# gMLP: u by seven block products a chunk pair, spatial mixing as fp32 products, modulation steps in two out-projections

## The chip, the cores and the metric

One core of one Trainium2 chip runs the whole program. The time is device microseconds of one execution; the kernel before has a median of 2796.57 us over three runs (2794.27 to 2799.32). TensorE (PE) multiplies, VectorE (DVE) and ScalarE (ACT) work elementwise, GpSimd (POOL) and SyncE (SP) issue DMAs, POOL also reduces over partitions.

## The reference, cut to what matters

Two layers over 512 latent and 256 context tokens (768 rows of width 1024, all fp32). Each layer is FFN, token mixer, FFN; every sub-layer is modulated by shift, scale and gate that come from a conditioning vector. The mixer of layer 0 is the one that changes:

```python
def gmlp_mix(h, w_in, sgu_g, sgu_b, w_s, b_s, w_out):      # h: (1, T, 1024)
    u, v = jnp.split(jax.nn.gelu(h @ w_in, approximate=False), 2, axis=-1)   # 3072 each
    v = layer_norm(v, sgu_g, sgu_b)
    v = v.reshape(b_, t_ // 128, 128, 8, 384)
    v = jnp.einsum('gpq,bnqgc->bnpgc', w_s, v) + b_s.T[None, None, :, :, None]
    return (u * v.reshape(b_, t_, 3072)) @ w_out
m = jax.nn.silu(cond) @ w_mod + b_mod                       # modulation, nine vectors a layer
```

The spatial product mixes the 128 tokens of a chunk of tokens with one 128x128 matrix w_s for each of eight groups of 384 channels.

## The kernel before, in words

**Precision.** Matrix products run on fp32r data. Each fp32 operand is split into a high part (an ACT cast) and a low part (a DVE subtraction), and each product is made of three: high x high, high x low, low x high (`split`, `split_later`, `product`). So every weight tile costs a cast of 128x512 on ACT and a subtraction of 128x512 on DVE. Where text says "the low part of a weight", this subtraction is meant.

**Sub-layers.** In order: FFN 0, gMLP, FFN, FFN, attention, FFN. An FFN and gMLP's v use a seven-product scheme (Strassen and Winograd's) over blocks of h: features in two halves, tokens in two halves of 384. Its operands made from h are called B11, T1, T2, B21, T3, B22, T4 (`combine`) and its weight sums come from four raw tiles g1, u1, u2, g2 (job kind "s" in `units`, lines 327 to 359: four DVE operations on the raw tiles, L334, L337, L345, L353, and seven splits). One tile makes 7 x 12 = 84 matmuls of 128x384.

**gMLP.** First the v stage: v for all tokens, written to DRAM (`v_spill`), with statistics for its norm. Then the u stage, a loop over 24 chunks j of 128 channels. A chunk (a) makes u by eight plain block products a token half (`project`, 96 matmuls of 128x384 for two chunks, weight jobs "u": two raw tiles a chunk, no sums); (b) fetches v's chunk from DRAM on SP's queue, scales it by the norm on ACT (`normed`, six operations of 128x128) and splits it (ACT 128x768, DVE 128x768); (c) mixes it (`spatial`): w_s, transposed and split, is a moving operand of 256 columns, v's high and low parts are the weights, 12 matmuls; (d) adds the two halves with gain and bias on DVE (six operations of 128x256), applies gelu to u on ACT and multiplies; (e) does one or two modulation steps. The results of the last KEPT = 4 chunks are split and stay on chip, those of the others go to DRAM by POOL's queue.

**Out-projections.** `out_proj` runs over the rows of the weights f (24 in gMLP, 22 in an FFN), once for each half of 512 output columns. A row is 6 token blocks x 3 = 18 matmuls of 128x512. Rows in DRAM are read back by POOL's queue (`feed`), split three rows ahead (`prepare`, AHEAD = 3), and weights are made up to eight tiles ahead (W_BUFS). The second half keeps READ_BACK = 10 rows from the first. DVE also does the residual (z by ln_g and ln_b) there.

**Modulation.** w_mod is not multiplied on TensorE: a modulation step (`mod_unit`, called by `fill`) loads 256 KB of w_mod on SP's queue and adds it, times one element of the conditioning vector, into an accumulator on DVE, once for each of two vectors. A unit (layer, index) has 16 steps; after eight, POOL reduces the accumulator over partitions. MOD_PLAN says which units belong to which sub-layer; what is left of them at the sub-layer's end is done there at once. Steps are placed by calls of `fill` in the loops.

**What sets the order.** From `pin(True)` on, every engine runs its instructions in the order in which the program writes them. `slot` sets it after each block product: low parts of weights waiting, an early copy, up to two new weight tiles, then the step's own work.

## Time and profile before

| | us |
|---|---|
| median of three runs | 2796.57 |
| the profiled execution | 2794.23 |
| its span on the chip | 2790.9 |
| TensorE busy | 2746.1 (98%) |
| DVE busy | 2078.2 (74%) |
| ACT busy | 1294.0 (46%) |
| u stage, first product to the out-projection's first | 732.78 to 970.40 |

Times in the views count from the span's start. L89 is the line of a helper that pins operations, so nearly every row has it; rows are told apart by the names out<-in: `ps<-comb,w` are block products on h, `ps<-w_sT,vn` spatial products, `ps<-w,acts` out-projections, `acc<-mraw` modulation steps. PE is TensorE's matmul, PEld its weight load, which overlaps. A matmul's own time contains its latency; what one costs in a row of many is the distance from start to start.

### The profile page before, as it was taken

To read this page: it belongs to the slowest core of one execution; us is meant where nothing else is said; L and a number is where in the kernel's file an instruction comes from. 1 tells how busy PE (TensorE), PEld (TensorE's weight loads), DVE (VectorE), ACT (ScalarE), POOL (GpSimd) and SP (SyncE) were. 2 spreads that over 40 slices of the span, in tenths; PEclk is the share of its full clock that TensorE was granted. 3 is DMA by queue.
4 is the path that set the end of the run, shared out by engine and by line. 5 is a ranking of instruction groups with operands and counts; after the bars stand their busy time and mean duration, and the time that the engine had idled before them with its cause. 6 is when DMAs were issued, how large, how long until landed. Compare 5 with 4: busy or idle time off the path is not lost.

```text
span 2790.9 us, 41006 instructions
## 1 busy us (share of the span) xinstructions
PE 2746.1 (98%) x14370; PEld 2481.2 (89%) x14370; DVE 2078.2 (74%) x3601; ACT 1294.0 (46%) x2559; POOL 548.6 (20%) x620
## 2 busy tenths in 40 slices
PE   7999999999999999999999999999999999999998
PEld 5999988888899988899998889999988888888887
DVE  6879989587798876587898659789896698733445
ACT  6544442475655432564444246444432666623321
POOL 1002144212111241100314120013242121000001
PEclk9999999999999999999999999999999999999999
DMA  7444466377766483344456534454594424354352
GB/s 234 142 138 143 138 235 207 111 223 231 220 191 178 131 291 108 119 148 148 137 146 218 174 105 144 144 147 141 170 313 148 148 72 91 130 151 130 112 170 87
DMA packets 408133, 447.31 MB, mean 160 GB/s; under 512 B 29560, under 2 KB 289080, under 8 KB 407928
## 3 DMA queue, kind: packets, MB, share of 16 engines
q1 hardware_dynamic: 371848, 332.77, 38.3%
q0 software_dynamic: 36080, 111.93, 13.2%
q8 instruction: 112, 1.84, 0.3%
q14 instruction: 93, 0.76, 0.1%
HBM read 382.62 MB, written 64.19 MB: 160 GB/s over the span
## 4 chain that ended last, share of the span: by engine, by line
PE 65%; DVE 3%; ACT 2%; issue 2%; POOL 1%; DMA 0%; SPq 0%; DVEq 0%; POOLq 0%; ACTq 0%
PE ps L89 64%; PE pp L89 1%; ACT h L692 0%; POOL rs L203 0%; ACT z L2228 0%; ACT p L1743 0%; DVE nm L1735 0%; DVE z L89 0%; DVE q L1640 0%; DMA mraw<-in_w_mod_dram 0%; POOL acc L474 0%; DVE ss L1609 0%; ACT comb L706 0%; ACT w L172 0%; DVE w L89 0%
## 5 line engine op out<-in xcount | busy, mean ns | idle before, releaser
L89 PE MATMUL ps<-comb,w 128*128 128x384 f32 x6696 | 1172.9, 335 | 5.2 <-DVE w L89 2.5
L89 PEld LDWEIGHTS ps<-comb,w 128*128 128x128 f32 x6696 | 1160.4, 188 | 8.9 <-DVE w L89 3.8
L89 PE MATMUL ps<-w,acts 128*128 128x512 f32 (+1 forms) x3792 | 861.1, 388 | 3.6 <-DVE q L89 3.6
L89 PEld LDWEIGHTS ps<-w,acts 128*128 128x128 f32 x3792 | 707.1, 188 | 149.4 <-DVE q L89 4.5
L89 DVE TENSOR_TENSOR w<-raw,w 128x512 fp32r<-128x512 f32 x643 | 470.7, 740 | 288.0 <-ACT w L89 286.5
L89 ACT CAST w<-raw 128x512 fp32r<-128x512 f32 x643 | 395.1, 621 | 625.2 <-PE ps L89 543.8
L89 DVE SCALAR_TENSOR_TENSOR acc<-mraw,cs,acc 128x512 f32<-128x512 f32 x392 | 280.9, 752 | 23.8 <-DMA mraw<-in_w_mod_dram 23.5
L474 POOL PARTITION_ALL_REDUCE acc<-acc x56 | 205.0, 3666 | 327.2 <-DVE acc L89 300.4
L89 PE MATMUL ps<-h,w 128*128 128x512 f32 (+1 forms) x1152 | 241.4, 372 | 0.2 <-DVE w L173 0.2
L89 PEld LDWEIGHTS ps<-h,w 128*128 128x128 f32 x1152 | 203.2, 188 | 37.7 <-DVE w L173 0.4
L89 POOL DMA_DIRECT2D act<-stage x84 | 48.3, 575 | 903.2 <-DVE stage L89 863.7
L89 POOL DMA_DIRECT2D q<-act x226 | 128.2, 615 | 424.3 <-DVE acts L89 252.6
L89 ACT COPY q<-ps 128x384 f32<-128x384 f32 (+1 forms) x182 | 87.9, 483 | 203.0 <-PE ps L89 203.0
L89 PE MATMUL ps<-w,comb 128*128 128x512 f32 x756 | 173.9, 391 | 1.4 <-ACT ps L89 0.8
L89 DVE TENSOR_TENSOR w<-sums,w 128x512 fp32r<-128x512 f32 x198 | 140.8, 717 | 45.7 <-ACT w L89 45.7
L89 PEld LDWEIGHTS ps<-w,comb 128*128 128x128 f32 x756 | 141.2, 188 | 32.5 <-ACT ps L89 1.8
L89 ACT CAST acts<-q 128x384 fp32r<-128x384 f32 (+1 forms) x262 | 127.6, 519 | 71.1 <-DMA q<-act 54.3
L89 DVE TENSOR_TENSOR acts<-q,acts 128x384 fp32r<-128x384 f32 (+1 forms) x262 | 148.7, 604 | 11.3 <-ACT acts L89 11.0
L89 ACT CAST w<-sums 128x512 fp32r<-128x512 f32 x198 | 122.8, 622 | 40.9 <-DVE sums L353 22.2
L203 POOL TENSOR_TENSOR rs<-ve,mhalf 128x1 f32<-128x1 f32 (+3 forms) x47 | 38.5, 820 | 281.3 <-DVE ve L200 181.2
L173 DVE TENSOR_TENSOR w<-raw,w 128x512 fp32r<-128x512 f32 x101 | 67.3, 688 | 24.5 <-ACT w L172 24.1
L89 DVE TENSOR_TENSOR q<-q,ps 128x384 f32<-128x384 f32 (+1 forms) x69 | 39.6, 574 | 58.0 <-PE ps L89 58.0
(223 smaller groups left out, 2528.8 us busy)
## 6 DMA issues: line engine op xcount, KB each, us to landing
raw<-in_ffn_w_in_dram SPq DMA_DIRECT2D x400, 256.0 KB
mraw<-in_w_mod_dram SPq DMA_DIRECT2D x256, 256.0 KB
raw<-in_ffn_w_out_dram SPq DMA_DIRECT2D x176, 256.0 KB
q<-act POOLq DMA_DIRECT2D x216, 192.0 KB, 4.5
raw<-in_gmlp_w_in_dram SPq DMA_DIRECT2D x132, 256.0 KB
act<-stage POOLq DMA_DIRECT2D x74, 384.0 KB, 3.1
zhat<-z POOLq DMA_DIRECT2D x26, 512.0 KB, 3.0
raw<-in_gmlp_w_out_dram SPq DMA_DIRECT2D x48, 256.0 KB
```

The costliest lines, as they stand in the source:

```text
L89: return self.tc.keep_in_program_order(f(*args, **kwargs))
L173: self.lows.append((key, lambda: self.dve.tensor_tensor(lo, src, hi.bitcast(F32), ALU.subtract)))
L203: self.last_rstd = self.nc.gpsimd.tensor_tensor(rs, ve, self.mhalf[:, 0:1].to_broadcast([P, n]), ALU.pow).ins
L474: nc.gpsimd.partition_all_reduce(accs[c], accs[c], P, bass_isa.ReduceOp.add)
```

## The change

u goes through the same seven products as the FFN's tiles, two chunks at a time: the pair's first chunk stands where the gate tile stands, the second where the up tile stands, and the sums of h that the v stage made (T1, T2, T3, B22, T4) are used again, so B12 and the kept copy of h are dropped. A pair reads its four raw weight tiles as a job of kind "s": seven splits and four sums in place of four splits. The spatial product takes v unsplit in fp32, with w_s transposed but unsplit as a moving operand of 128 columns: six matmuls a chunk, each into its own 128 columns of two of four banks set aside. The sum over w_s's columns (`ones`) becomes fp32 too. Adding gain and bias is two DVE operations of 128x384 in place of six of 128x256. v's ring has four places instead of three. The loop holds no modulation steps: unit (0, 6) moves to the first sub-layer, whose out-projection does an additional step in rows 1, 3 and 6 of every eight (before: row 3), and gMLP's out-projection does additional ones (`acts.ring`). Two chunks stay on chip instead of four, and the first half of the out-projection begins with chunks 0, 1, 2, which are read back during the last pairs.

Removed lines that the listing above shows are mostly left out.

```diff
@@ -58,6 +58,7 @@
 KEPT, READ_BACK = 4, 10
+KEPT_MIX, READ_BACK_MIX = 2, 10
...
 MOD_PLAN = [
-    [(0, 2), (0, 3), (0, 4), (0, 5)],
-    [(0, 6), (0, 7), (0, 8)],
+    [(0, 2), (0, 3), (0, 4), (0, 5), (0, 6)],
+    [(0, 7), (0, 8)],
...
-        def through(wo, n):
-            for half, order in enumerate(Acts.orders(n, KEPT, READ_BACK)):
+        def through(wo, n, keep=KEPT, back=READ_BACK):
+            for half, order in enumerate(Acts.orders(n, keep, back)):
                 jobs.append(("u", [piece(wo, f, half) for f in order]))
...
         us = lambda j: [wi[:, 4 * half : 4 * half + 4, j * P : j * P + P] for half in range(2)]
-        for j in range(GMLP_CH):
-            jobs.append(("u", us(j)))
-        through(io["gmlp_w_out"][0], GMLP_CH)
+        for j in range(0, GMLP_CH, 2):
+            (g1, g2), (u1, u2) = us(j), us(j + 1)
+            jobs.append(("s", [g1, u1, u2, g2]))
+        through(io["gmlp_w_out"][0], GMLP_CH, KEPT_MIX, READ_BACK_MIX)
...
-    def combine(self, keep=False):
+    def combine(self):
...
-        orders = acts.orders(n, KEPT, READ_BACK)
+        orders = acts.order
...
                 elif residual and x > 2 and (half or x % 2):
                     residual.pop(0)()
-                    self.fill(int(self.light))
+                    self.fill(int(self.light or acts.ring and x % 4 == 1))
                 elif half or x < n - 1:
                     self.fill_pair()
-                    if prev is None and x % 8 == 3:
+                    if prev is None and x % 8 in (1, 3, 6) or acts.ring and x % 8 in (2, 6):
                         self.fill()
...
-    def gmlp_v(self, room, spill, vst, early_group, late_group):
+    def gmlp_v(self, room, spill, vst):
...
         act, dve = self.act, self.dve
-        self.combining = self.combine(True)
-        sets = [[self.bank(("v", x, t)) for t in range(HALF)] for x in range(2)]
+        self.combining = self.combine()
+        sets = [[self.bank(("v", x, t), True) for t in range(HALF)] for x in range(2)]
...
     def gmlp(self, l, i, nblocks, end, prev):
...
+        room = self.box("v", F32)
+        self.gmlp_v(room, spill, vst)
...
+        acts = Acts(self, GMLP_CH, TOK, KEPT_MIX, READ_BACK_MIX, f"act{l}{i}_")
+        acts.ring = True
+        store = self.main.tile([P, 2 * D], F32, tag="gate", bufs=1, name="S")
+        S = [store[:, x * TOK : x * TOK + TOK] for x in range(2)]
+        bias = store[:, 2 * TOK : 2 * TOK + 4 * P].rearrange("p (n t) -> p n t", n=4)
+        ring = room[:, :].rearrange("p (n b t) -> p n b t", n=4, b=NB)
+        T1, T2 = slice(0, HT), slice(HT, TOK)
...
+        for x in range(4):
+            self.bank(("mix", x))
+        mix_order = [self.bank_held["mix", x] for x in range(4)]
+
+        def mix_bank():
+            x = mix_order.pop(0)
+            mix_order.append(x)
+            return self.psum.tile([P, 512], F32, tag=f"ps{x}", bufs=1, name="ps")
...
-            ps = self.bank()
+            ps = mix_bank()
             self.tp(ps[:, 0:P], ws_raw.pop(g))
-            wT = self.main.tile([P, 2, P], F32R, tag="sums", bufs=2, name="w_sT")
-            self.split(wT[:, 0], wT[:, 1], ps[:, 0:P])
+            wT = self.zplace()[:, 0:P]
+            act.copy(wT, ps[:, 0:P])
             yield
-            ps = self.bank()
-            self.mm(ps[:, 0 : 2 * P], self.ones, wT, True, True)
+            ps = mix_bank()
+            self.mm(ps[:, 0:P], self.ones, wT, True, True)
             dve.tensor_copy(r, ps[:, 0:P])
-            dve.tensor_tensor(r, r, ps[:, P : 2 * P], ALU.add)
             yield wT, r, bs
...
         def fetch(j):
             if j < GMLP_CH:
...
+                self.sp.dma_start(ring[:, j % 4], src)
+
+        def normed(j, bs=range(NB)):
+            v = ring[:, j % 4]
+            for b in bs:
+                act.activation(v[:, b], v[:, b], AF.Identity, bias=nb[:, b : b + 1], scale=rs[b])
...
+        def v_stats():
             for b in range(NB):
+                dve.bn_aggr(mv[:, b], vst[b])
+            r = self.rstd(mv[:, :, 1], NB)
+            rs.extend(r[:, b : b + 1] for b in range(NB))
+            self.v_rs = r
+
+        def v_bias():
+            dve.scalar_tensor_tensor(nb, mv[:, :, 0], -1.0, self.v_rs, ALU.mult, ALU.mult)
+
+        self.following = group(0)
+        late = []
+        kept = {}
+
+        def spatial(j):
+            if j % 3 == 0:
+                self.grp = self.grp_next
+                self.following = group(j // 3 + 1) if j // 3 + 1 < GMLP_GROUPS else iter((None, None, None))
+            wT, r, bs = self.grp
+            self.grp_next = next(self.following)
+            if j % 3 == 2:
+                load_ws(j // 3 + 2)
+            v = ring[:, j % 4]
+            banks = [mix_bank(), mix_bank()]
+            for b in range(NB):
+                o = (b % HALF) * P
+                self.mm(banks[b // HALF][:, o : o + P], v[:, b], wT, True, True)
+            fetch(j + 4)
+            box = []
+
+            def mixed(x):
+                if not x:
+                    base = self.sm([P], "base", 2)
+                    sc = self.sguT[:, GMLP_CH + j : GMLP_CH + j + 1]
+                    dve.scalar_tensor_tensor(base, r, sc, bs, ALU.mult, ALU.add)
+                    box.append(base[:, :].unsqueeze(1).to_broadcast([P, HALF, P]))
+                cut = lambda t: t.rearrange("p (b t) -> p b t", t=P)
+                out = cut(S[j % 2][:, x * HT : x * HT + HT])
+                gain = self.sguT[:, j : j + 1]
+                dve.scalar_tensor_tensor(out, cut(banks[x][:, 0:HT]), gain, box[0], ALU.mult, ALU.add)
+
+            late.extend([lambda: mixed(0), lambda: mixed(1)])
+
+        def times(j, cols, u):
+            if not cols.start:
+                kept[j] = acts.place(j)
+            m, done = kept[j]
+            to = u if m is None else m[:, cols]
+            dve.tensor_tensor(to, u, S[j % 2][:, cols], ALU.mult)
+            done(cols, to)
+
+        def step(ps, name, go_on, early, *posts):
+            self.product(ps, name, go_on)
+
+            def post():
+                for f in posts:
+                    f()
+                for _ in range(2):
+                    if late:
+                        late.pop(0)()
+
+            self.slot(post, 2, 0, early)
+            self.release(1)
+
+        add = lambda out, a, b: dve.tensor_tensor(out, a, b, ALU.add)
+        gelu = lambda out, src: act.activation(out, src, AF.Gelu)
+        nothing = lambda: None
+        load_ws(0)
+        load_ws(1)
+        for j in range(4):
             fetch(j)
...
+        next(self.following)
+        for a in range(0, GMLP_CH, 2):
+            begin, final = not a, a == GMLP_CH - 2
+            seeded = self.part_bank(marked=True)
+            b1, g = self.part_bank(), self.acc()[:, 0:HT]
+            step(b1, "B11", False, lambda: act.copy(seeded, b1), v_stats if begin else lambda: normed(a))
+            if begin:
+                next(self.following)
+            if final:
+                self.filler_raw()
+            b2, p5 = self.part_bank(), self.acc()[:, 0:HT]
+            step(b2, "T1", False, None, lambda: act.copy(p5, b2), v_bias if begin else nothing)
+            if final:
+                acts.prepare(0, 0)
+            v, w = self.q(512)[:, 0:HT], self.q(512)[:, 0:HT]
+            half = (lambda j, x: lambda: normed(j, range(HALF * x, HALF * x + HALF))) if begin else lambda j, x: nothing
+            step(seeded, "T2", True, None, lambda: act.copy(v, seeded), half(0, 0))
+            if final:
+                acts.prepare(0, 1)
+            step(b1, "B21", True, None, lambda: gelu(g, b1), half(0, 1))
+            if begin:
+                self.grp_next = next(self.following)
+            else:
+                spatial(a)
+                late.append(lambda: times(a, T1, g))
+            if a >= GMLP_CH - 4:
+                acts.feed(0, 2)
+            step(seeded, "T3", True, lambda: act.copy(w, seeded), half(1, 0) if begin else lambda: normed(a + 1))
+            step(b2, "B22", True, None, lambda: add(v, v, b2), lambda: add(w, w, p5), half(1, 1))
+            if not begin:
+                spatial(a + 1)
+            x = self.acc()[:, 0:HT]
+            if final:
+                acts.prepare(0, 2)
+
+            def last():
+                gelu(v, v)
+                gelu(w, w)
+                gelu(x, seeded)
+
+            step(seeded, "T4", True, None, last)
+            if begin:
+                spatial(a)
+                late.append(lambda a=a, g=g: times(a, T1, g))
+                late.append(lambda a=a, v=v: times(a, T2, v))
+                spatial(a + 1)
+            else:
+                late.append(lambda a=a, v=v: times(a, T2, v))
+            late.append(lambda a=a, x=x: times(a + 1, T1, x))
+            late.append(lambda a=a, w=w: times(a + 1, T2, w))
+        while late:
+            late.pop(0)()
+        for x in range(4):
+            self.unhold(("mix", x))
         self.out_proj(acts, l, i, 1.0, end, prev)
...
-        self.ones = const.tile([P, P], F32R, name="ones")
+        self.ones = const.tile([P, P], F32, name="ones")
...
     def __init__(self, k, n, ntok, keep, back, name):
         self.k, self.n, self.ntok, self.back = k, n, ntok, back
-        self.per, self.keep, self.free = 3072 // (2 * ntok), keep, n - keep
+        self.per, self.keep, self.free, self.ring = 3072 // (2 * ntok), keep, n - keep, False
...
     def orders(n, keep, back):
 
         kept, free = list(range(n - keep, n)), list(range(n - keep))
-        return kept + free, free[-back:] + free[:-back] + kept
+        early = 0 if keep > AHEAD else AHEAD
+        return free[:early] + kept + free[early:], free[-back:] + free[:-back] + kept
...
         if f < self.free:
             x = f % (2 * self.per)
-            if not x:
+            if not f or not x and not self.ring:
                 self.stage = k.box("stage", F32)
```

The program's order, on the engines that wait or are waited for, at three places.

TensorE in the middle of the u stage (comb,w are products of u, v and vn spatial products). Before, three chunks' pieces:

```order
L89 MATMUL ps<-comb,w 128x384 x48
L89 MATMUL ps<-ident,s_7538 128x128
L89 MATMUL ps<-w_sT,vn 128x256 x12
L89 MATMUL ps<-comb,w 128x384 x48
L89 MATMUL ps<-w_sT,ones 128x256
```

With the change, one pair and the beginning of the next:

```order
L90 MATMUL ps<-comb,w 128x384 x60
L90 MATMUL ps<-ident,s_7563 128x128
L90 MATMUL ps<-zraw,v 128x128 x6
L90 MATMUL ps<-comb,w 128x384 x24
L90 MATMUL ps<-zraw,ones 128x128
L90 MATMUL ps<-zraw,v 128x128 x6
L90 MATMUL ps<-comb,w 128x384 x60
```

Of a pair's 84 products 24 (T3, B22) stand between its two spatial chunks and 60 (T4, then B11, T1, T2, B21 of the next pair) behind the second; before, a chunk's 48 stood between any two.

ACT in the same place; `v<-v` is the scaling of v. Before, one chunk:

```order
L89 ACTIVATE su<-ps 128x384 x2
L89 ACTIVATE v<-v,v_nb,rs_7246 128x128 x6
L89 CAST vn<-v 128x768
L89 CAST w<-raw 128x512 x2
L89 CAST w_sT<-ps 128x128
```

With the change, from the gelu that follows B21 on, through T3, B22, T4 and the next pair's B11:

```order
L90 ACTIVATE acc<-ps 128x384
L90 COPY q<-ps 128x384
L90 CAST w<-raw 128x512
L90 ACTIVATE v<-v,v_nb,rs_7301 128x128 x6
L90 CAST w<-sums 128x512
L90 COPY zraw<-ps 128x128
L90 CAST w<-raw 128x512
L90 ACTIVATE q<-q 128x384 x2
L90 ACTIVATE acc<-ps 128x384
L90 COPY ps<-ps 128x384
L90 CAST w<-raw 128x512
L90 ACTIVATE v<-v,v_nb,rs_7301 128x128 x6
```

The scaling of the pair's second chunk stands behind the copy that waits for T3 and one cast; that of the first behind the copy that waits for B11 and one cast.

DVE in the first half of gMLP's out-projection (acts are rows being split, z<-z,zraw the residual, acc<-mraw modulation steps). Before:

```order
L89 SCALAR_TENSOR_TENSOR acc<-mraw,cs,acc 128x512 x2
L89 TENSOR_TENSOR w<-raw,w 128x512
L89 TENSOR_TENSOR acts<-q,acts 128x384 x2
L89 TENSOR_TENSOR z<-z,zraw 128x512 x2
L89 TENSOR_TENSOR w<-raw,w 128x512
```

With the change:

```order
L90 SCALAR_TENSOR_TENSOR acc<-mraw,cs,acc 128x512 x4
L90 TENSOR_TENSOR w<-raw,w 128x512
L90 TENSOR_TENSOR acts<-q,acts 128x384 x2
L90 TENSOR_TENSOR z<-z,zraw 128x512 x2
L90 SCALAR_TENSOR_TENSOR acc<-mraw,cs,acc 128x512 x2
L90 TENSOR_TENSOR w<-raw,w 128x512
```

Two steps stand in some rows that had one, and one in some residual rows that had none.

145 lines of the change are left out of this document (7 added, 138 removed).

## The prediction

> **What bounds the kernel now.** I read the page first, then busy time by stage, then TensorE's own order of time in the stage that changes.
>
> ```profile
> PE 2746.1 (98%) x14370; PEld 2481.2 (89%) x14370; DVE 2078.2 (74%) x3601; ACT 1294.0 (46%) x2559; POOL 548.6 (20%) x620
> ...
> core 0: us, PE busy (x) PEld busy (x) DVE busy (x) ACT busy (x) POOL busy (x), PEclk, DMA share, GB/s
> 60.00:371.70 311.70, 311.70 (x1802) 311.02 (x1801) 265.66 (x420) 156.50 (x314) 46.87 (x41) 1.00 0.46 136
> 735.00:976.00 241.00, 239.61 (x1468) 238.24 (x1467) 202.62 (x412) 125.50 (x274) 49.65 (x43) 1.00 0.57 170
> ```
>
> TensorE works in 2746 of 2791 us. In the u stage (735 to 976) it has no hole but one, and its clock is granted in full, so what this stage is worth is the sum of TensorE's products, as long as the other engines keep up. The FFN stage (60 to 371.7) matters as a witness: it already makes seven block products a tile, with DVE at 265.66 / 311.70 = 85%, and TensorE never stops.
>
> TensorE alone, in order of time (start, duration, count; a bracket gives idle time):
>
> ```profile
> 732.78 16.82 PE L89 MATMUL ps<-comb,w 128*128 128x384 f32 x96
> 749.44 1.59 PE L89 MATMUL ps<-w_sT,vn 128*128 128x256 f32 x12
> ...
> 753.48 0.73 PE L89 MATMUL ps<-w_sT,vn 128*128 128x256 f32 x4 [1.39 <-ACT su L89]
> ...
> 762.37 0.28 PE L89 MATMUL ps<-w_sT,ones 128*128 128x256 f32 x1
> 762.49 1.60 PE L89 MATMUL ps<-w_sT,vn 128*128 128x256 f32 x12
> 763.93 8.52 PE L89 MATMUL ps<-comb,w 128*128 128x384 f32 x48
> 772.28 1.59 PE L89 MATMUL ps<-w_sT,vn 128*128 128x256 f32 x12
> 773.71 8.49 PE L89 MATMUL ps<-comb,w 128*128 128x384 f32 x48
> 782.04 0.27 PE L89 MATMUL ps<-ident,s 128*128 128x128 f32 x1
> ...
> 970.40 14.92 PE L89 MATMUL ps<-w,acts 128*128 128x512 f32 x65
> ```
>
> From start to start: 48 products of u take 772.28 - 763.93 = 8.35 us (174 ns each), the 12 spatial products 763.93 - 762.49 = 1.44 us (120 ns each). The stage runs from 732.78 to 970.40 = 237.6 us. Check: 24 x (8.35 + 1.44) = 235.0, the 1.39 hole, and about 1.2 for eight transposes and sums of w_s.
>
> **Products of u (the gain).** A chunk pair has 96 products of 128x384 now and 7 x 12 = 84 after. Nothing else about them changes. 12 pairs x 12 x 0.174 = 25.1 us less; the u products come to 12 x 84 x 0.174 = 175.4 us.
>
> **Spatial products (the unknown).** Instead of 12 split products of 256 columns a chunk there are 6 fp32 products of 128 columns, and w_s is summed over by eight more: 152 in all. The trace of before has no unsplit fp32 product. The nearest rows are the split product above, 256 columns at 120 ns, and the fp32 transpose:
>
> ```profile
> 1161.68 1.05 PE L89 MATMUL ps<-ident,z 128*128 128x128 f32 x8
> ...
> L89 PE MATMUL ps<-ident,z 128*128 128x128 f32 x272 | 36.8, 278 | 0.8 <-DMA z<-in_x_dram 0.8
> ```
>
> Eight transposes end 1.05 us after the first starts and one lasts about 0.28, so they follow at (1.05 - 0.28) / 7 = 110 ns: fp32 data loaded as 128 weights, 128 columns streamed once. The built program of the change counts 14,234 matmuls and as many weight loads for 14,082 products, so each of the 152 becomes two. Low end: two transposes, 220 ns. If each of the two streams its 128 columns twice, it is a 256-column product of 120 ns: 240 ns. [...] Sum: 24 x 1.44 + 8 x (0.24 + 0.08) = 37.1 us. [...]
>
> [...]
>
> So TensorE's stage is 175.4 + 37.1 = 212.5 us against 237.6: 25.1 less, the hole of 1.39 among it, since the new loop starts with products that need no v.
>
> **The stage's start and its queues.** v's chunks are read back from DRAM by SP; the first one arrives late in both kernels:
>
> ```profile
> 741.14 1.26 ACT L1504 ACTIVATE v<-v,v_nb,rs 128x128 f32<-128x128 f32 x3 [6.98 <-DMA v<-v_spill]
> ```
>
> That is 8.4 us into the stage; the new loop's first spatial product comes after seven block products, at 14.6. Later a fetch stands on SP's queue behind the spatial products that free its place in the ring of four, and the weight loads stand behind the fetch; they are wanted a pair (17.7 us) later, and a fetch two pairs later, so I cost the wait at nothing; without this lead a fetch would cost TensorE those 7 us. The dropped copy of part of h and the dropped split of v relieve engines that did not hold TensorE: nothing.
>
> **DVE in the new stage.** Rows for the pieces of one pair:
>
> ```profile
> L89 DVE TENSOR_TENSOR w<-raw,w 128x512 fp32r<-128x512 f32 x643 | 470.7, 740 | 288.0 <-ACT w L89 286.5
> L334 DVE TENSOR_TENSOR sums<-raw 128x512 f32<-128x512 f32 x66 | 45.4, 689 | 11.9 <-DMA raw<-in_ffn_w_in_dram 11.3
> L89 DVE TENSOR_TENSOR q<-q,ps 128x384 f32<-128x384 f32 x57 | 31.3, 550 | 8.8 <-PE ps L89 8.8
> L89 DVE SCALAR_TENSOR_TENSOR su<-ps,sguT,s 128x256 f32<-128x256 f32 x72 | 31.7, 480 | 13.3 <-PE ps L89 11.5
> L89 DVE SCALAR_TENSOR_TENSOR s<-v,sguT 128x128 f32<-128x128 f32 x24 | 8.8, 367 | 0.0
> L89 DVE TENSOR_TENSOR stage<-su 128x384 f32<-128x384 f32 x40 | 24.0, 640 | 0.0
> ```
>
> Seven low parts of weights at 0.74, four weight sums at 0.69, two adds at 0.55, four gain-and-bias steps of 384 columns (between 0.48 for 256 and 0.69 for 512: 0.6), two bases at 0.37, four products with u at 0.64: 5.2 + 2.8 + 1.1 + 2.4 + 0.7 + 2.6 = 14.8 us in a pair of 212.5 / 12 = 17.7, 84%. That is the witness's 85%, so it hides. Without the cover it would be the bound only above 17.7.
>
> **ACT in the new stage.** ACT has more here than in any stage now, and its order matters: v is scaled in place on ACT, and the spatial products wait for it.
>
> ```profile
> 861.46 2.41 ACT L89 ACTIVATE v<-v,v_nb,rs 128x128 f32<-128x128 f32 x6
> ...
> L89 ACT CAST w<-raw 128x512 fp32r<-128x512 f32 x643 | 395.1, 621 | 625.2 <-PE ps L89 543.8 <-issue 53.7 <-DVE raw L89 15.0
> L89 ACT COPY q<-ps 128x384 f32<-128x384 f32 (+1 forms) x182 | 87.9, 483 | 203.0 <-PE ps L89 203.0
> L89 ACT ACTIVATE su<-ps 128x384 f32<-128x384 f32 x48 | 22.7, 493 | 67.3 <-PE ps L89 67.3
> ```
>
> Seven casts at 0.62, four copies at 0.48, four gelus at 0.49, two scalings of 2.41: 13.0 of 17.7, 74%. For the even chunk the scaling is issued after B11, three products ahead of its use. For the odd chunk it stands behind the copy that follows T3 and one cast, and its user comes one product later, after B22: TensorE is ready at 12 x 0.174 = 2.1 us past T3, while ACT ends the first block at about 0.48 + 0.62 + 0.49 = 1.6 and one more every 0.4, the sixth at 3.6. TensorE wants its sixth at 2.1 + 5 x 0.24 = 3.3. It waits some 0.3 us, in 11 pairs at most 3; I take 2.
>
> **Modulation steps moved.** A step is two DVE operations (1.41 us together), one 256 KB load on SP's queue, and every eighth step two all-reduces on POOL. By the loops, the u stage loses 33 steps; the first FFN's out-projection gets 16 more (5 of them in its first half), gMLP's 17 more (11 in its first half). What these two do now:
>
> ```profile
> 372.00:458.00 86.00, 86.00 (x380) 70.93 (x379) 74.37 (x112) 30.70 (x61) 43.76 (x47) 1.00 0.81 278
> 978.00:1066.00 88.00, 88.00 (x389) 72.62 (x388) 65.82 (x113) 30.84 (x62) 28.74 (x42) 1.00 0.74 255
> 1048.56 0.62 ACT L89 CAST w<-raw 128x512 fp32r<-128x512 f32 x1 [2.63 <-PE ps L89]
> 1049.82 1.02 DVE L89 TENSOR_TENSOR acts<-q,acts 128x384 fp32r<-128x384 f32 x2
> 1052.64 0.62 ACT L89 CAST w<-raw 128x512 fp32r<-128x512 f32 x1 [2.63 <-PE ps L89]
> 1054.84 1.41 DVE L89 SCALAR_TENSOR_TENSOR acc<-mraw,cs,acc 128x512 f32<-128x512 f32 x2
> ...
> DVE acc L89 <- DMA mraw<-in_w_mod_dram: 8.0, 1, 8.0
> ```
>
> A row of the weights takes 4.08 us there (1052.64 - 1048.56). The first halves get 5 steps (7 us of DVE) and 11 (15.5 us): 81 of 86 and 81 of 88, the latter 83 with the two more rows that are reread (2 x 1.0). That is 94%, and a row with two steps has 0.7 + 1.0 + 2.8 = 4.5 us of work; but activations are made three rows ahead (12 us) and weights up to eight, and the next row is lighter. Loads go from 278 to 278 + 5 x 0.26 MB / 86 us = 293 GB/s in the one, and from 255 to 255 + (11 x 0.26 + 0.8) / 88 = 297 GB/s in the other. I take 1 us for both.
>
> **Sum.** 25.1 - 2 - 1 = 22 us less. The profiled execution took 2794.23 us (span 2790.9), the median of the runs is 2796.57, 2.3 more. 2796.6 - 22 = 2774.5: I say **2774 us**.
>
> **Rivals.**
> [...]
> Second, the odd chunk's wait is larger: ACT stands behind the copy after T3, and DVE's lag delays the bank that a spatial product overwrites. Should ACT reach the scaling only when B22 ends, 1.0 us later than worked out, its sixth block is ready at 2.1 + 0.49 + 5 x 0.4 = 4.6 where TensorE wants it at 3.3: 1.3 us a pair, 14 in 11 pairs, 12 more than the 2 counted: 2786. For it: 74% on an in-order queue that waits for each product; against: TensorE has two products' slack everywhere else, and the FFN's same loop has none lost.
> Third, the out-projections, at 94% DVE and nearly 300 GB/s, where DVE already waited once for 8 us for a modulation load (last row above), hold TensorE: two rows late in each, 8 us: 2782. Against: nothing of that wait reached TensorE.
>
> **How the numbers follow.** Forecast 0.65, with a range of its own of 2767 to 2781; first rival 0.14, second 0.14, third 0.07. 0.2% is 5.6 us, about what the measurement can tell from no change. Faster: 0.63 + 0.12 + 0.06 of forecast, second and third, 0.81; slower: 0.12 of the first rival; same: the other 0.07, where a rival's price comes out near the point from which it decides. Low end of the range: 2774, less 3 for the low fp32 price, less 3 for no waits of ACT and the out-projections, less 4 for the spread of the runs: 2764. The high end takes in the second and third rival and some of the way to the first, at an fp32 price of 385 ns: 2797.
>
> **What would show it.** In the changed profile: u's products at 12 x 84 with 174 ns from start to start; a spatial chunk of 1.4 us (2.6 or more means the first rival); the stage 212 to 216 us long; idle time before the spatial products put down to ACT's v under 3 us; both out-projections as long as now, at 93 to 95% DVE in their first halves. It is wrong if the six products of a chunk take over 2.3 us, or if TensorE's busy share in the stage falls under 97%.

## The result, and the profile after

The changed kernel takes 2816.09 us (median of four runs, 2813.58 to 2817.10) against 2796.69 us: 1.0068 of the time before, 95% interval 1.0050 to 1.0085. It is slower by 19.4 us where 22 less were forecast. The profiled execution took 2813.58 us, its span 2811.8.

The page of the changed kernel:

```profile
PE 2737.7 (97%) x14234; PEld 2464.8 (88%) x14234; DVE 2086.1 (74%) x3554; ACT 1314.4 (47%) x2624; POOL 555.8 (20%) x627
```

Its busy time in three stretches that were shown of before (columns as there):

```profile
372.00:458.00 86.00, 72.31 (x305) 58.73 (x304) 71.55 (x105) 26.57 (x53) 46.08 (x49) 0.92 0.77 267
735.00:976.00 241.00, 231.71 (x1369) 222.69 (x1368) 167.74 (x311) 151.50 (x346) 22.50 (x40) 0.99 0.51 158
978.00:1066.00 88.00, 87.78 (x395) 72.84 (x394) 77.88 (x122) 32.48 (x68) 41.18 (x48) 1.00 0.75 247
```

TensorE has 8.4 us less work than before and the span is 20.9 us longer. The first stretch shows where: in the first out-projection TensorE works 72.31 of 86 us (86.00 before), and its granted clock is 0.92. TensorE in order of time, the rows with a hole and one pair of the u stage:

```profile
406.82 28.52 PE L90 MATMUL ps<-w,acts 128*128 128x512 f32 x124 [1.81 <-DVE acts L90]
447.23 0.28 PE L90 MATMUL ps<-ident,s 32*128 32x32 f32 x1 [11.88 <-DMA s<-mod]
...
559.23 1.97 PE L90 MATMUL ps<-ident,z 128*128 128x128 f32 x8 [5.29 <-ACT z L2239]
...
753.96 2.27 PE L90 MATMUL ps<-comb,w 128*128 128x384 f32 x12
759.68 0.33 PE L90 MATMUL ps<-ident,s 128*128 128x128 f32 x1 [3.45 <-DMA s<-in_gmlp_w_s_dram]
...
795.91 8.59 PE L90 MATMUL ps<-comb,w 128*128 128x384 f32 x48 [0.58 <-ACT acc L90]
804.34 0.27 PE L90 MATMUL ps<-ident,s 128*128 128x128 f32 x1
804.45 1.50 PE L90 MATMUL ps<-zraw,v 128*128 128x128 f32 x12
805.71 4.41 PE L90 MATMUL ps<-comb,w 128*128 128x384 f32 x24
809.95 0.38 PE L90 MATMUL ps<-zraw,ones 128*128 128x128 f32 x2
810.17 1.75 PE L90 MATMUL ps<-zraw,v 128*128 128x128 f32 x12
811.68 2.35 PE L90 MATMUL ps<-comb,w 128*128 128x384 f32 x12
814.62 8.59 PE L90 MATMUL ps<-comb,w 128*128 128x384 f32 x48 [0.58 <-ACT acc L90]
...
982.12 0.86 PE L90 MATMUL ps<-w,acts 128*128 128x512 f32 x3
1087.07 84.15 PE L90 MATMUL ps<-w,acts 128*128 128x512 f32 x360 [4.58 <-DVE q L90]
```

`ident,s` at 447 is the transpose of a modulation unit's columns, the one at 759 that of w_s. The distances between TensorE's milestones, from each kernel's profiled execution, with the same for the runs below:

| us | first out-projection to u stage | u stage | gMLP's out-projection to the first transpose of z | from there to TensorE's last matmul |
|---|---|---|---|---|
| before | 361.1 | 237.6 | 181.3 | 1628.0 |
| forecast | 361.6 | 214.5 | 181.8 | 1628.0 |
| after | 382.2 | 228.2 | 188.9 | 1629.3 |
| move_alone | 383.4 | 237.7 | 183.7 | 1627.1 |
| turn_later | 379.1 | 228.4 | 188.5 | 1629.5 |
| no_reduce | 360.5 | 229.7 | 181.9 | 1627.0 |
| thin_additions | 365.3 | 227.9 | 181.9 | 1625.2 |
| early_end | 382.5 | 228.6 | 188.9 | 1628.6 |
| bank_order | 387.1 | 216.7 | 189.7 | 1628.5 |
| ws_early | 382.4 | 226.7 | 187.5 | 1630.2 |
| fp32_alone | 362.4 | 234.4 | 181.4 | 1629.9 |
| unit_back | 362.1 | 229.1 | 183.9 | 1631.2 |
| combined | 365.4 | 215.8 | 189.6 | 1631.7 |
| three_fixes | 364.0 | 215.8 | 183.4 | 1631.1 |

So the change wins 9.4 us in the u stage and loses 21.1 and 7.6 in the two out-projections. Two cautions belong to the table. In bank_order, combined and three_fixes the stage's first product waits 1.39 us for ScalarE's `q`, and the first column has this wait. The last column goes from 1625.2 to 1631.7, though most of the runs change nothing there, so 2 or 3 us between two traces say little.

A hole costs more than its own length, as the granted clock (last but two) in the changed kernel's windows shows:

```profile
407.00:409.00 2.00, 2.00 (x10) 1.62 (x11) 2.00 (x4) 0.00 (x0) 1.70 (x4) 1.00 0.00 0
449.00:451.00 2.00, 2.00 (x6) 1.53 (x5) 2.00 (x5) 0.00 (x0) 0.00 (x0) 0.50 0.70 230
453.00:456.00 3.00, 3.00 (x13) 2.40 (x13) 2.88 (x5) 1.30 (x3) 2.85 (x1) 0.91 0.60 203
1089.00:1091.00 2.00, 2.00 (x6) 1.60 (x5) 1.68 (x3) 0.00 (x0) 2.00 (x1) 0.50 0.00 0
```

Behind the hole of 1.81 us the clock stays at 1.00; behind those of 11.88 and 4.58 it is 0.50 for 6.3 and 4.8 us, with six matmuls in 2 us where there are ten otherwise. The length of a hole alone does not decide: one of 3.57 us before 2028.84 in this trace left the clock at 1.00, while behind that of 3.45 before 759.68 it is 0.50 from 761 to 763. The holes up to the u stage, 19.2 us less the 2.2 that before has there, and some 4.8 of half clock make 21.8, for the 21.1 lost. In gMLP's out-projection the hole of 4.58 and 2.4 of half clock make 7.0 of the 7.6.

### The profile page after: what moved, and what is told of

Same layout as the page of the kernel before. It is cut to its first block, busy times and chain, and to the rows that moved or that the text cites. A ratio compares the mean times of both kernels' runs of the same rounds, so it can differ in the third digit from the quotient of the medians.

```text
span 2811.8 us, 40725 instructions
## 1 busy us (share of the span) xinstructions
PE 2737.7 (97%) x14234; PEld 2464.8 (88%) x14234; DVE 2086.1 (74%) x3554; ACT 1314.4 (47%) x2624; POOL 555.8 (20%) x627
## 4 chain that ended last, share of the span: by engine, by line
PE 78%; DVE 6%; issue 5%; ACT 4%; DMA 4%; POOL 3%; SPq 0%; DVEq 0%; POOLq 0%; ACTq 0%
PE ps L90 77%; POOL acc L476 2%; DVE acc L90 1%; DVE w L90 1%; DMA mraw<-in_w_mod_dram 1%; ACT w L90 1%; DMA q<-act 1%; PE pp L90 1%; DVE acts L90 1%; DMA raw<-in_w_mod_dram 1%; ACT z L2239 1%; DVE z L90 0%; DVE q L90 0%; ACT h L694 0%; DMA acc<-in_gmlp_w_in_dram 0%
## 5 line engine op out<-in xcount | busy, mean ns | idle before, releaser
L90 PE MATMUL ps<-comb,w 128*128 128x384 f32 x6552 | 1156.1, 336 | 11.4 <-ACT acc L90 5.8
L90 PEld LDWEIGHTS ps<-comb,w 128*128 128x128 f32 x6552 | 1137.8, 188 | 18.4 <-ACT acc L90 9.0
L90 DVE TENSOR_TENSOR w<-sums,w 128x512 fp32r<-128x512 f32 x234 | 165.3, 711 | 69.2 <-ACT w L90 69.0
L90 POOL DMA_DIRECT2D q<-act x234 | 134.1, 638 | 405.3 <-DVE acts L90 270.5
L90 ACT COPY q<-ps 128x384 f32<-128x384 f32 (+1 forms) x206 | 99.4, 483 | 237.3 <-PE ps L90 237.2
L90 DVE TENSOR_TENSOR acts<-q,acts 128x384 fp32r<-128x384 f32 (+1 forms) x270 | 160.2, 628 | 14.6 <-ACT acts L90 14.3
L90 ACT CAST w<-sums 128x512 fp32r<-128x512 f32 x234 | 144.8, 620 | 45.2 <-DVE sums L355 23.3
L90 DVE TENSOR_TENSOR q<-q,ps 128x384 f32<-128x384 f32 (+1 forms) x81 | 46.1, 570 | 58.7 <-PE ps L90 58.6
```

The lines of the kernel that those rows point to most:

```text
L90: return self.tc.keep_in_program_order(f(*args, **kwargs))
```

## The experiments

**1. The move alone.** In the kernel before, the plan of units and the rules for additional steps were taken from the change (with gMLP's out-projection told by its 24 rows), and the u loop's steps removed (one line that issues the next steps' loads near the loop's end stands in their place):

```diff
-    [(0, 2), (0, 3), (0, 4), (0, 5)],
-    [(0, 6), (0, 7), (0, 8)],
+    [(0, 2), (0, 3), (0, 4), (0, 5), (0, 6)],
+    [(0, 7), (0, 8)],
...
-                    if prev is None and x % 8 == 3:
+                    if prev is None and x % 8 in (1, 3, 6) or n == GMLP_CH and x % 8 in (2, 6):
...
-            self.fill(int(0 < j < GMLP_CH - 1) * (2 - j % 2))
```

> The kernel before, with only the modulation steps moved as in the change: none in the u stage, unit (0, 6) in the first out-projection, the rest in gMLP's. First theory: the move alone makes both out-projections longer, by what the changed kernel's trace shows there: the u stage starts 21.2 us later (753.96 against 732.78) and gMLP's out-projection takes 7.6 us more (188.9 against 181.3), so 2796.7 + 28.8 = 2825 us, and TensorE's wait for the modulation columns of 11.9 us, for z of 5.3 and for q of 4.6 are there again. Rival: these waits come from something else in the change (the other order of rows, the weights' jobs, the places of accumulators in the new loop); then the move alone stays within 4 us of before, 2793 to 2801.

Measured: 2818.23 us, 1.0076 of before (1.0061 to 1.0091), 22.4 more. What TensorE waited for between 360 and 760 us:

```profile
PE ps L89 <- DMA s<-mod: 11.0, 1, 11.0
PE ps L89 <- ACT z L2229: 6.0, 1, 6.0
PE ps L89 <- DVE acts L89: 2.2, 1, 2.2
...
```

The first out-projection's loss is the move's, whole: 383.4 us here, 382.2 in the changed kernel, 361.1 before. Of gMLP's 7.6 us the move alone brings 2.3; there the same steps cost 1.8 to 5.8 us of wait at the half's boundary from one run to the next (`DVE q`), and what sets it was not found.

**2. The sums over partitions left out.**

```diff
             for c in range(nconds):
-                nc.gpsimd.partition_all_reduce(accs[c], accs[c], P, bass_isa.ReduceOp.add)
                 nc.gpsimd.dma_start(m[c : c + 1, s], accs[c][0:1, :], accum_op=ALU.add)
```

> The changed kernel, without GpSimd's sums of the accumulators over partitions (56 of them in the whole program; one partition's partial sum is sent in place of the sum, so this part of the computation is left out). First theory: the steps cost the out-projections more than their own 1.41 us of VectorE, since VectorE's operations that overlap such a sum are longer by 100 us in all (1.8 us a sum), and GpSimd's next other operation after one came 6.8 us late at the end of the first out-projection. Without them the waits for z (5.3 us and 1.8 of half clock) and for q (4.6 and 2.4) vanish and the one for the columns shrinks by the two sums of 9 us that precede it: 14 to 25 us less, 2791 to 2802. Rival: the steps' own additions and loads set the waits, and the sums matter only to the wait for z: 7 us less, 2809 or more.

Measured: 2784.75 us, 0.9952 of before (0.9936 to 0.9969): 31.3 less than the changed kernel, with every step still in its row. Both out-projections are as long as before the change. TensorE's waits from 370 to 760 us:

```profile
PE ps L90 <- DMA s<-in_gmlp_w_s_dram: 3.7, 1, 3.7
PE ps L90 <- DMA s<-mod: 2.0, 1, 2.0
PE ps L90 <- DVE w L90: 0.2, 1, 0.2
...
```

The 3.7 us for w_s belong to the u stage; ahead of it TensorE waits 2.4 us, against 2.2 in the kernel before. So without the sums the steps' own additions and loads, all that the prediction had costed, cost next to nothing. What a sum does to VectorE, its rows of the changed kernel show in gMLP's out-projection:

```profile
1045.34 1.02 DVE L90 TENSOR_TENSOR acts<-q,acts 128x384 fp32r<-128x384 f32 x2
...
1054.33 3.69 DVE L90 TENSOR_TENSOR acts<-q,acts 128x384 fp32r<-128x384 f32 x2
```

GpSimd at that time (POOL; `mod<-acc` is the DMA that sends a sum off):

```profile
1048.47 5.78 POOL L476 PARTITION_ALL_REDUCE acc<-acc  x1
...
1055.13 3.47 POOL L476 PARTITION_ALL_REDUCE acc<-acc  x1
```

The same two operations take 1.02 us alone and 3.69 beside a sum. In the whole trace 62 of VectorE's operations last over 0.3 us longer than the median of their kind, and 60 of these overlap one of the 56 sums; the excess is 100 us, 1.8 a sum. In the run without sums one such operation is left. The kernel before has 56 sums too, with 99 us of excess: the change moved sums, it added none. Delayed are operations on two SBUF tensors and those on one with a scalar, though not at each overlap: 19 of the 42 low parts of raw weights (`w<-raw,w`) that overlap a sum, and 19 of the 22 operations that begin an accumulator (`acc<-mraw,cs`). The accumulating steps themselves (25 overlaps) and the drains of PSUM (12) were never late by over 0.3 us in this trace. Two SBUF tensors alone do not decide it, since these steps read two as well; what does, no run shows.

**3. The additions thinned, the sums kept.** Experiment 2 does not part VectorE's lateness from GpSimd's own time: two sums, 5.20 and 3.46 us, also stand directly in the path of the columns that TensorE waited 11.9 us for. So the reverse was run, with all additions but the first of each eight cut from 512 columns to 8:

```diff
-                        dve.scalar_tensor_tensor(accs[c], raw, cs, accs[c], ALU.mult, ALU.add)
+                        dve.scalar_tensor_tensor(accs[c][:, 0:8], raw[:, 0:8], cs, accs[c][:, 0:8], ALU.mult, ALU.add)
```

> The changed kernel with every modulation step's addition cut from 512 columns to 8, but for the first of each eight (that part of the computation is left out); loads, sums over partitions and the places of all of them stay. It parts VectorE's lateness from GpSimd's queue as the way by which the sums cost the out-projections. Theory one: VectorE is full, with the steps' 1.41 us each and 1.8 us a sum on top; with some 1.2 us a step gone it is on time, the units are ready earlier, and all waits in the out-projections go but the one for z (GpSimd's own switch, 5.3 us and 1.8): 2816.1 - 11.9 - 3.5 - 1.8 - 4.6 - 2.4 = 2792. Theory two: GpSimd's queue and the way of the columns through DRAM are late by themselves, whatever VectorE does: the wait of 11.9 us stays at over 8, 2808 or more.

Measured: 2784.91 us, 0.9957 of before (0.9943 to 0.9971); 7 better than theory one said. TensorE's waits from 370 to 760 us:

```profile
PE ps L90 <- DMA s<-in_gmlp_w_s_dram: 3.2, 1, 3.2
PE ps L90 <- DMA s<-mod: 3.0, 1, 3.0
PE ps L90 <- ACT z L2239: 1.9, 1, 1.9
...
```

The sums still delay VectorE here, by 85 us in the whole trace, but the first out-projection takes 365.3 us, 4.2 more than before the change in place of 21.1. With the sums and nearly without the additions, or with the additions and without the sums, VectorE keeps up; with both it does not. In the changed kernel it is full in stretches, one in each out-projection ahead of the hole:

```profile
400.00:435.00 35.00, 33.19 (x147) 26.93 (x145) 34.79 (x44) 9.65 (x19) 26.38 (x25) 1.00 0.63 205
...
1070.00:1080.00 10.00, 10.00 (x45) 8.01 (x44) 9.93 (x19) 1.56 (x3) 0.00 (x0) 1.00 0.65 207
```

In the kernel before, VectorE was busy for 33.66 us of the first of these stretches, so it was nearly full there already, and for 5.81 of the ten as far into gMLP's out-projection as the second.

**4. The transposes put off.** A unit's columns are transposed on TensorE's in-order queue a fixed number of steps after its last sum. With more steps a row that place came forward from row 18 to row 14.

```diff
-        self.later(TURN_LATER - READ_LATER, finish)
+        self.later((8 if (l, i) == (0, 3) else TURN_LATER) - READ_LATER, finish)
```

> The changed kernel, with TensorE's transposes of the first unit's columns put off from row 14 to row 17 of the first out-projection; nothing else moved. First theory: they stand too early on TensorE's queue, since their place counts modulation steps and there are now more steps in a row; 11.9 us of idle time and the half-speed clock behind it (6 to 7 us at 0.5, so 3.5) vanish: 2816.1 - 15 = 2801. Rival: VectorE is so far behind there that TensorE stops at the same place for the next thing VectorE makes (activations, weights): less than 5 us is won, 2811 or more.

Measured: 2809.80 us, 1.0044 of before (1.0029 to 1.0059), 6.3 less. TensorE's waits from 370 to 600 us:

```profile
PE ps L90 <- ACT z L2239: 5.5, 1, 5.5
PE ps L90 <- DVE acts L90: 4.7, 3, 2.3
PE ps L90 <- DVE q L90: 3.5, 1, 3.5
...
```

The 11.9 us are gone and 6.4 of them are back: 2.9 more for activations and 3.5 for the banks of the first half. In the profiled execution the stage is 3.1 us shorter. Neither theory had it; the place was wrong, and VectorE was late as well.

**5. The last sum earlier.** In the second half the additional steps go to rows 7 to 11.

```diff
-                    if prev is None and x % 8 in (1, 3, 6) or acts.ring and x % 8 in (2, 6):
+                    if prev is None and (x in (7, 8, 9, 10, 11) if half else x % 8 in (1, 3, 6)) or acts.ring and x % 8 in (2, 6):
```

> The changed kernel, with the last steps of unit (0, 6) done in rows 7 to 11 of the first out-projection's second half, so that its last sum over partitions stands behind row 11 in place of row 14; as many steps as now. First theory: the wait for z at the end comes from GpSimd, which needs 6.8 us from the last sum's DMA to the small power operation that the norm waits for; three rows (12 us) earlier it is ready in time: 5.3 us of wait and 1.8 of half clock less, 2816.1 - 7 = 2809. Rival: VectorE is late for the last block as such, and the denser steps keep it so: 2814 or more.

Measured: 2815.56 us, 1.0063 of before (1.0048 to 1.0079), nothing won. GpSimd in the changed kernel:

```profile
545.77 3.44 POOL L476 PARTITION_ALL_REDUCE acc<-acc  x1
549.51 0.80 POOL L477 DMA_DIRECT2D mod<-acc  x1 [0.30 <-POOL acc L476]
557.12 0.59 POOL L204 TENSOR_TENSOR rs<-ve,mhalf 128x1 f32<-128x1 f32 x1 [6.81 <-issue]
```

Its input was ready at 551.1; the 6.81 us with no wait in them lie between a sum and the next operation of another kind. In the run, with the sum three rows earlier, the wait for z is gone. This does not confirm the theory, since TensorE stood still for 6.2 us ahead of it and the operation's input came late for that reason (9.91 us after GpSimd's last issue). That standstill has its cause in GpSimd's queue, which also reads the rows back:

```profile
534.85 7.34 POOL L476 PARTITION_ALL_REDUCE acc<-acc  x1 [5.44 <-DVE acc L90]
...
543.08 3.44 POOL L476 PARTITION_ALL_REDUCE acc<-acc  x1
...
547.36 1.41 POOL L90 DMA_DIRECT2D q<-act  x2
```

The last rows' reads now stand behind the last sums, which start at 534.85; in the changed kernel the last one was issued at 530.2, ahead of them. TensorE waits 6.2 us for these activations where it waited 5.3 for z:

```profile
PE ps L90 <- ACT acts L90: 6.2, 1, 6.2
```

**6. Another bank for B11.**

```diff
-            seeded = self.part_bank(marked=True)
             b1, g = self.part_bank(), self.acc()[:, 0:HT]
+            seeded = self.part_bank(marked=True)
```

> The changed kernel, with a pair's first bank taken before the seeded one, so that B11 no longer overwrites the bank that T4 has just filled. First theory: TensorE starts B11 0.83 us late in 11 pairs (2.94 us from T4 to B11 where twelve products take 2.11), because gelu has to read that bank first; with another bank that goes: 9.1 us, 2816.1 - 9 = 2807, and a pair takes 17.9 us in place of 18.7. Rival: ScalarE's queue as such is late, and the wait moves to the next product that needs a copy of it (T2 on the seeded bank, or the odd chunk's scaling): 2814 to 2816.

Measured: 2806.16 us, 1.0030 of before (1.0020 to 1.0040), 9.9 less. TensorE, a pair from T4 to T4:

```profile
794.43 10.66 PE L90 MATMUL ps<-comb,w 128*128 128x384 f32 x60
804.93 0.27 PE L90 MATMUL ps<-ident,s 128*128 128x128 f32 x1
805.04 1.50 PE L90 MATMUL ps<-zraw,v 128*128 128x128 f32 x12
806.30 4.41 PE L90 MATMUL ps<-comb,w 128*128 128x384 f32 x24
...
812.27 10.67 PE L90 MATMUL ps<-comb,w 128*128 128x384 f32 x60
```

All eleven waits are gone, and a pair takes 812.27 - 794.43 = 17.84 us; the prediction had 17.7. The u stage is 11.5 us shorter: 9.1 are these waits, and the rest is mainly w_s's hole, 1.97 us in place of 3.45 and with 36 products in 6.35 us behind it in place of 7.91. Against that, the stage's very first product now waits 1.39 us for its bank. The first out-projection, which the edit does not touch, is some 3.5 us longer in this trace.

**7. The first w_s earlier.** Its load is issued in the v stage, behind the T2 of its last pair of tiles:

```diff
...
             step(x, "T2", True, keep(u2))
+            if seed is None:
+                early_group()
...
```

> The changed kernel, with the load of the first w_s issued in the v stage, ahead of raw weights that SyncE's queue waits for; nothing else. First theory: TensorE's wait of 3.45 us after the first twelve products, and half a microsecond to one of slow clock behind it, come from that load being issued at 756.1, 2.2 us after the stage's start: 2816.1 - 4 = 2812. Rival: the next thing that comes late at the start (v, or the bank that the transpose writes) takes its place: 2815 to 2817.

Measured: 2812.14 us, 1.0050 of before (1.0036 to 1.0064), 4.0 less. The w_s wait is gone, but 2.23 of its 3.45 us are back as a wait for VectorE's `S` in the middle of the second spatial chunk. The u stage of the profiled execution is only 1.5 us shorter (226.7), so it is in part luck that the total came out at the theory's 2812.

**8. The fp32 products alone.** In the kernel before; v is scaled into the room of its split parts, and the sums of w_s and the additions of gain and bias are as in the change.

```diff
...
-                    self.mm(o, vn[:, 0, b], wT, True, False)
-                    self.mm(o, vn[:, 1, b], wT, False, True)
+                    self.mm(ps[:, h * P : (h + 1) * P], vn[:, bb * HALF + h], wT, True, True)
...
```

> The kernel before, with only the spatial products and the sums of w_s changed: v unsplit in fp32, six products of 128 columns a chunk, and two additions of 128x384 in place of six of 128x256. First theory: the price seen in the changed kernel (1.26 us for a chunk's six, 210 ns each) holds here too, 24 x (1.26 - 1.44) = 4.3 us less and some tenths for the eight sums: 2796 - 4.5 = 2791.5. Rival: the price depends on what the chunk's products stand between, and among products of 128x384 in this order they cost the 240 ns that the prediction took or more: no change, 2796 or above.

Measured: 2795.03 us, 0.9990 of before (0.9981 to 0.9999); the u stage is 3.3 us shorter. TensorE there:

```profile
801.09 1.50 PE L89 MATMUL ps<-w_sT,vn 128*128 128x128 f32 x12
802.35 8.57 PE L89 MATMUL ps<-comb,w 128*128 128x384 f32 x48
```

1.26 us for six products again, 210 ns each, though they stand between other products here. The total moved by 2.7 of the 4.5 us, at the edge of what can be told.

**9. Unit (0, 6) back in the u stage.**

```diff
-    [(0, 2), (0, 3), (0, 4), (0, 5), (0, 6)],
-    [(0, 7), (0, 8)],
+    [(0, 2), (0, 3), (0, 4), (0, 5)],
+    [(0, 6), (0, 7), (0, 8)],
...
-                    if prev is None and x % 8 in (1, 3, 6) or acts.ring and x % 8 in (2, 6):
+                    if prev is None and x % 8 == 3 or acts.ring and x % 8 in (2, 6):
...
+            piece = self.acc if begin or a >= GMLP_CH - 4 else lambda: self.q(512)
+            steps = int(2 <= a < 18)
...
             step(b2, "T1", False, None, lambda: act.copy(p5, b2), v_bias if begin else nothing)
+            self.fill(steps)
...
+            self.fill(steps)
             if a >= GMLP_CH - 4:
                 acts.feed(0, 2)
```

g, p5 and x are taken from `piece`.

> The changed kernel, with unit (0, 6) taken out of the first out-projection, which is then as before, and put into the u stage: two steps a pair in eight pairs (the pair's short-lived pieces stand in another ring there, so that the accumulators have theirs alone). First theory: the first out-projection was what cost 21.2 us, and the u stage has room: VectorE works 12.9 us of a pair's 18.7 there, two steps are 2.8, four sums over partitions in eight pairs 4 x 1.8 / 8 = 0.9, together 16.6. So 2816.1 - 21 = 2795, the u stage as long as now, 228 us. Rival: on an in-order queue with 89% of its time taken, VectorE is late for what TensorE waits for, 1 us or more a pair: 2803 or more.

Measured: 2792.20 us, 0.9978 of before (0.9969 to 0.9987). The first out-projection is as before (362.1), and the u stage, with 16 steps and four sums more, is 229.1 us against 228.2.

**10 and 11. Versions with the causes removed.** First four repairs together: the bank order, unit (0, 6) in the u stage, the early w_s, and a fourth, which was

```diff
-                    self.fill(int(self.light or acts.ring and x % 4 == 1))
+                    self.fill(int(self.light or acts.ring and not half and x < 16 and x % 4 == 1))
...
-                    if prev is None and x % 8 == 3 or acts.ring and x % 8 in (2, 6):
+                    if prev is None and x % 8 == 3 or acts.ring and (8 <= x < 14 if half else x < 16 and x % 8 in (2, 6)):
```

> The changed kernel with four things: the bank order of the run before, unit (0, 6) in the u stage (as in the run of that name), the load of the first w_s issued in the v stage, and in gMLP's out-projection no additional steps in the last third of the first half (they move to rows 8 to 13 of the second). First theory, from the waits each removes: 2816.1 - 21.2 (first out-projection as before) - 9.1 (bank) - 4.5 (w_s: 3.45 of wait and 1 of slow clock) - 7 (q at the boundary: 4.6 and 2.4) = 2774, faster than the kernel before by 0.8%. Rival: with pairs of 17.9 us in place of 18.7, VectorE's 16.6 are 93%, and half of what the bank gave comes back as waits for VectorE; and the sums over partitions move their cost to the second half: 2783 or more.

Measured: 2787.29 us, 0.9966 of before (0.9954 to 0.9979), 13 above the theory. Three parts did most of what they were to do (365.4 us with the 1.39 of the first product, and 215.8), the fourth harm: TensorE's waits from 950 to 1190 us were 4.9 for `ACT acts`, with sums at 1094 to 1104 and 1117 to 1125 ahead of the row reads, as in experiment 5. Without it:

> The combined version without its fourth part: gMLP's out-projection has the changed kernel's steps in their rows again; bank order, unit (0, 6) in the u stage and the early load of w_s stay. First theory: thinning the end of the first half did harm, since two pairs of sums over partitions 16 us apart in the second half stood ahead of the rows that GpSimd's queue reads back (4.9 us of wait for activations there, 189.6 us up to the first transpose of z against 183.9 with the steps where the change has them): 2787.3 - 5.7 = 2781.6. Rival: with the u stage's pairs at 17.9 us, gMLP's out-projection starts with less in hand, and it loses as much at the half's boundary (4.6 and 2.4 us in the changed kernel): 2787 to 2789.

Measured: 2780.31 us (2779.18 to 2781.44, five runs), 0.9937 of before (0.9923 to 0.9950): 0.6% under the kernel before, and 35.8 us under the changed one. Busy time in its u stage, VectorE at 179.45 of 217 us:

```profile
735.00:952.00 217.00, 214.33 (x1319) 211.31 (x1318) 179.45 (x323) 145.58 (x339) 37.57 (x44) 1.00 0.60 186
```

and what TensorE still waits for from 950 to 1190 us:

```profile
PE ps L90 <- DVE q L90: 1.8, 1, 1.8
PE ps L90 <- DVE w L90: 1.3, 2, 0.7
```

The forecast was 2774 us. The first three stages of the table come to 763.2 us here, and in the forecast to 757.9.

## Why the prediction was wrong

**Products of u: right.** 48 take 804.34 - 795.91 = 8.43 us in the changed kernel, 176 ns each: 177.0 us for 1008, forecast 175.4.

**The fp32 price: right in kind, a little high.** 210 ns, below the low end of 220. Each product is two instructions; what each does inside, no run shows. The 240 ns of the forecast's sum are shown by no run; in their place the runs showed 210 ns, 1.26 us for a chunk's six: 24 x 1.26 + 8 x 0.32 = 32.8 us against 37.1. At 210 ns, against the 385 of the range's high end, the first rival is out.

**The odd chunk: as described, twice the size.** ScalarE's scaling of it ends at 811.39, and TensorE's six products run from 810.17 to 811.68: 1.51 us, in other pairs up to 1.78, against 1.26 for the even one: 4.3 us in eleven pairs where 2 were taken.

**The start, costed at nothing: 5.0 us.** The first w_s was issued behind raw weights that SyncE waits for, and 3.45 us of hole and a half-speed clock behind it, 1.6 more, followed. The prediction looked at v's chunks in that queue and not at w_s.

**A wait it did not have: B11, 9.1 us.** From T4 to the next B11 the trace has 814.62 - 811.68 = 2.94 us where twelve products take 2.11. The second rival named a bank that a lagging engine frees late, but for the spatial products and VectorE. It was the pair's own rotation: three of four banks a pair, so that B11's bank was the one T4 had filled last. With experiment 6 the stage is 216.7 us, or 218.1 with the wait of its first product, for a forecast of 214.5. The stage adds up: 177.0 + 32.8 + 4.3 + 9.1 + 5.0 = 228.2.

**The step that failed: "That is 94% ... I take 1 us for both"; the two out-projections lost 28.7 us.** Two things were wrong in it. The first is the cost of a step. The prediction counted its sums as work of GpSimd, which has time; in the trace each takes 1.8 us of VectorE, so eleven steps more bring 2.75 sums (two for eight steps), 4.9 us beside their own 15.5, and by the prediction's own count 83 of 88 becomes 88 of 88. The average of the window came out lower, 77.88, which says little: steps, sums and rows meet in stretches that are full (9.93 of 10 us, and 34.79 of 35 in the first out-projection). Experiments 2 and 3 show that it takes both: without the sums the first out-projection loses nothing, without the additions 4.2 of the 21.1 us. How much of the 11.9 us came from VectorE's delays and how much from the sums' own time in the path of the columns, they do not part. The second is that the buffers of three rows cannot help where something stands at a fixed place on TensorE's in-order queue. The transposes of the columns and the drain of the banks at the half's boundary have no rows in hand, and counting places in steps had moved the former four rows forward; experiment 4 put them back three rows, and 5.5 of the 11.9 us of wait went. The prediction followed steps, loads and the queues of SP and POOL, but not what a step's count moves on TensorE. The third rival had the place (out-projections held by VectorE) at 8 us; the DMA load that it leaned on was not the cause, since without the sums the same loads cost nothing. gMLP's out-projection takes 181.9 us without the sums, and without the additions too; why the same steps cost 2.3 us there in the move alone and 7.6 in the changed kernel stays open.

**GpSimd's 6.81 us after a sum, worth 7 us (5.3 of wait for z and 1.8 of half clock), were not seen.** In the kernel before, the same operation came 24 us after GpSimd's last issue and waited for its input alone, so nothing of them could be seen there.

Its own tests read rightly: a spatial chunk of 1.26 and 1.5 to 1.8 us is under 2.3, and TensorE's share fell to 231.71 / 241 = 96% in the window shown and to 218.87 / 228.16 = 96% in the stage itself, under the 97% that it had named.

## What to carry to other kernels

When work is moved into a stage, count everything that comes with it on every engine, the rare part too: here the rare sums, 1.8 us each on an engine that does not run them, tipped a load that the 1.41 us steps alone did not. Then look for what has a fixed place on the bottleneck's in-order queue (a transpose, a drain, the next user of a bank): slack in buffers does not reach it, and a place counted in moved items moves with them. Read an engine's load in short stretches too: an average of 86% (74.37 of 86 us) held one of 96% (33.66 of 35) in the kernel before. A stage with 31% of VectorE free, as the new u stage (115.8 of 168.4 us between 796 and 964, 12.9 a pair where 14.8 were forecast), is the better home for such work.

## What the runs showed of the hardware

- A sum over partitions on GpSimd (3.45 us, the first of a pair up to 7.3) delays many of VectorE's operations on SBUF, 1.8 us a sum, up to 2.7 for one operation; in the changed kernel the 12 drains of PSUM that overlapped one went free, and so did the 25 accumulating steps (in the kernel before one of 25 steps took 2.4 us longer).
- GpSimd's first operation of another kind after a sum started 6.81 us after the last DMA was issued, with no wait shown; in experiment 3 it was 7.00. What takes this time, no run shows.
- TensorE's granted clock fell to 0.50, for 3.4 to 6.3 us, after the four holes of 3.45 to 11.88 us shown above, and a hole of 4.6 us cost about 7. The length alone did not decide it: a hole of 3.57 us later in the same trace left it at 1.00. In experiment 3 the stretch from 371.7 to 460 us, whose one hole of 2.95 us ends at 435.79, has a mean clock of 0.98.
- An fp32 product of 128x128 by 128 columns takes 210 ns in a row of them, less than two fp32 transposes of the same size (220).
